# Gate products of a recurrent block: one fp32 matmul on whole tiles in place of three reduced-precision matmuls on split tiles

## The chip, the core and the metric

The kernel runs on one core of a Trainium2 chip. The metric is the device time of one execution in microseconds, as the median of several runs. A profile of one execution gives the instructions of each engine: TensorE (PE for its matmuls, PEld for its weight loads), VectorE (DVE), ScalarE (ACT), GpSimd (POOL) and SyncE (SP, which here issues the DMAs).

## What is computed

The reference is a trunk of two decoder layers on a sequence of 1024 positions with 1024 channels, all in fp32. Layer 0 mixes tokens with a gated linear recurrence (RG-LRU), layer 1 with stick-breaking attention; each is followed by a SwiGLU feed-forward network, and every sub-layer has an RMS norm before it and a residual add behind it. The change is in the recurrent block:

```python
def rg_lru_block(x, w_in, b_in, conv_w, conv_b, gate_w, gate_b, lam, w_out, b_out):
    u = jnp.einsum("bsd,de->bse", x, w_in) + b_in
    gate_branch, rec = u[..., :LRU_WIDTH], u[..., LRU_WIDTH:]
    rec = causal_depthwise_conv(rec, conv_w, conv_b)
    rec_blk = rec.reshape(bsz, seq, N_LRU_BLOCKS, LRU_BLOCK)
    gl = jnp.einsum("bsnc,gncd->gbsnd", rec_blk, gate_w).reshape(2, bsz, seq, LRU_WIDTH)
    gl = gl.astype(jnp.float32) + gate_b.astype(jnp.float32)[:, None, None, :]
    r_gate = jax.nn.sigmoid(gl[0])
    i_gate = jax.nn.sigmoid(gl[1])
    log_a = -LRU_C * r_gate * jax.nn.softplus(-lam.astype(jnp.float32))
    a = jnp.exp(log_a)
    mult = jnp.sqrt(-jnp.expm1(2.0 * log_a))
    b = mult * (i_gate * rec.astype(jnp.float32))
    _, h = lax.associative_scan(_linear_recurrence_combine, (a, b), axis=1)
    y = jax.nn.gelu(gate_branch, approximate=True) * h.astype(x.dtype)
    return jnp.einsum("bse,ed->bsd", y, w_out) + b_out
```

There are four blocks of 256 channels (N_LRU_BLOCKS, LRU_BLOCK), and the second einsum, `gl`, is two gates of four 256x256 products over all 1024 positions. It is this einsum that the change computes in another way.

## The kernel before

Activations lie with channels on the 128 partitions and positions along the free dimension, so 1024 channels are eight tiles of 128 x 1024, and a matmul moves half a tile, 512 positions, into one accumulator bank. Full precision is had from a reduced fp32 type (F32R): every operand is split into a high half, which is a cast to F32R, and a low half, the remainder, and `mm3` (lines 142 to 145) adds three matmuls, high by high, low by high and high by low. For weights, `load_raw` (line 113) brings 128 x 1024 numbers by DMA from the SP queue into one of three raw buffers (pool `rp`, tag `raw`); `split` (line 119) casts the high half on ScalarE (line 122) and subtracts for the low half on GpSimd (line 126). Both halves go into the weight ring (class `Ring`, line 67): six tiles of 128 x 1024 in two pools, four and two, handed out in turn, so that a tile is used again by the sixth allocation after it. A projection of 128 output channels takes two ring tiles and 48 matmuls (two halves, eight input tiles, three each).

The recurrent block runs its stages in the order written out in line 548, "A0 A1 B0 A2 G0 A3 Y0 B1 Y1 A4 G1 A5 B2 Y2 A6 G2 A7 B3 Y3 B4 Y4 G3 B5 Y5 B6 Y6", and `last_tile` after it. TensorE keeps this order; the other engines are ordered by a planner.

- `stage_a(e)` (line 471) projects the recurrent branch's tile e, scales it, and computes the causal convolution into `rec` (ScalarE line 478, three VectorE operations at line 480). Lines 481 to 484 split it into `rh` (ScalarE, line 482) and `rl` (VectorE, line 483); each of `rec`, `rh` and `rl` has three buffers.
- `stage_g(b)` (line 487), the gate block, covers the two channel tiles 2b and 2b+1. `load_gate` (line 442) loads both gates' weights by two DMAs into a raw buffer `rawg` (line 445) and splits them into two ring tiles. For each of two output tiles, two gates, two halves and two input tiles it calls `mm3` (line 498): 16 products, 48 matmuls, into `g_ps`. ScalarE and VectorE then do the activations and the scan of the recurrence (lines 504 to 515).
- `stage_b(e)` (line 518) projects the gate branch and applies GELU; `stage_y(e)` multiplies the two.

In each of the four gate blocks the tile `rec` is still needed after the products, at line 507. Behind the recurrent block come the output projection and the first feed-forward network, then attention and the second one; their weights go through the same ring (`wtile`, line 151), which is closed for attention (line 1352) and opened again behind it (line 1678).

Two other places use matmuls with F32 operands that aren't split: line 956 (sums of squares against a column of ones, eight products of one moving column each) and line 967 (a factor spread over the partitions, eight products of 128 moving columns); each is called once for either feed-forward network. Line 1559 in attention is a F32R matmul of 128 to 512 moving columns.

Of the kernel before, what the change touches and what calls it, by code (L numbers as in the profile page):

```python
# [8 lines left out]
F32 = mybir.dt.float32  # L9
F32R = mybir.dt.float32r  # L10
# [6 lines left out]
P = 128  # L17
S = 1024
D = 1024
# [14 lines left out]
def trunk(  # L34
# [22 lines left out]
    nc = tc.nc  # L57
    f32 = lambda t: t.bitcast(F32)

    cp = ctx.enter_context(tc.tile_pool(name="cp", bufs=1))  # L60
    rp = ctx.enter_context(tc.tile_pool(name="rp", bufs=3))
# [57 lines left out]
    def split(raw, pool=None, tag="w", bufs=None, lo_eng=None, parts=1):  # L119
        pool = pool or wpool[0]  # L120
        hi = pool.tile([P, D], F32R, tag=tag, name="whi", bufs=bufs)
        nc.scalar.copy(hi, raw)
        lo = pool.tile([P, D], F32R, tag=tag, name="wlo", bufs=bufs)
        for i in range(parts):
            c = slice(i * D // parts, (i + 1) * D // parts)
            (lo_eng or nc.gpsimd).tensor_sub(lo[:, c], raw[:, c], f32(hi)[:, c])
        return hi, lo
# [14 lines left out]
    def mm3(ps, wh, wl, mh, ml, first, last, **kw):  # L142
        nc.tensor.matmul(ps, lhsT=wh, rhs=mh, start=first, stop=False, **kw)  # L143
        nc.tensor.matmul(ps, lhsT=wh, rhs=ml, start=False, stop=False, **kw)  # L144
        nc.tensor.matmul(ps, lhsT=wl, rhs=mh, start=False, stop=last, **kw)  # L145
# [5 lines left out]
    def wtile(nm):  # L151
        return wpool[0].tile([P, D], F32R, tag="w", name=nm)
# [95 lines left out]
    half = lambda t, n: t[:, n * NB : (n + 1) * NB]  # L248
# [8 lines left out]
    with ExitStack() as st, tc.manual_schedule(engines={E.PE, E.Activation, E.DVE, E.Pool, E.SP}):  # L257
# [49 lines left out]
        ps = pst("vps0")  # L307
# [71 lines left out]
        for r0, r1 in ((0, 32), (32, 64), (64, P)):  # L379
            ps = pst("vps")  # L380
# [11 lines left out]
    with ExitStack() as st:  # L392
        lp = st.enter_context(tc.tile_pool(name="lp", bufs=1, reuse_waits="tile"))
        psl.append(lst.enter_context(tc.tile_pool(name="psB", bufs=2, space=PSUM, reuse_waits="tile")))
        V = nc.vector
        lam = vc[:, V_LAM : V_LAM + ND]
        sm = lambda name: lp.tile([P, ND], F32, name=name)
        V = nc.vector
# [38 lines left out]
        col = lambda base, i: vc[:, base + i : base + i + 1]  # L437
        ys = [lp.tile([P, S], F32, name=f"y{e}") for e in range(ND)]
        wide = lambda tag, bufs, dt=F32: lp.tile([P, S], dt, tag=tag, name=tag, bufs=bufs)
        rec, rech, recl, gel = {}, {}, {}, {}  # L440

        def load_gate(b):
            raw = rp.tile([P, D], F32, tag="raw", name="rawg")
            for g in range(2):
                nc.sync.dma_start(
                    raw[:, g * 512 : (g + 1) * 512].rearrange("p (k c) -> p k c", k=2),
                    gw[g, b].rearrange("(k p) c -> p k c", p=P),
                )
            hi, lo = split(raw)
            v4 = lambda t: t.rearrange("p (g k c) -> p g k c", g=2, k=2)  # L450
            return v4(hi), v4(lo)

        ahead = {0: aw[2], D + 2 * P: aw[3]}

# [3 lines left out]
        def ptile(name):  # L458
            turn[0] += 1
            i = (turn[0] - 1) // 2 % 2  # L460
            return psl[1 - i].tile([P, S], F32, tag="ba"[i], name=name)

        def project_col(c0):
            w = ahead.pop(c0) if c0 in ahead else load_cols(w_in, c0)
            ps = ptile("a_ps")
            for n in range(NH):
                project(ps, w, n)
            return ps


        def stage_a(e):
            ps = pa[e] if e < 2 else project_col(D + e * P)
            u = lp.tile([P, S + 16], F32, tag="u", name="u", bufs=2)
            V.tensor_copy(u[:, 0:3], nbias[:, e, 0:3])
            for n in range(NH):
                V.tensor_mul(u[:, 3 + n * NB : 3 + (n + 1) * NB], half(ps, n), rbc[n])
            rc = wide("rec", 3)
            nc.scalar.activation(rc, u[:, 3 : S + 3], AF.Identity, bias=cb[:, e : e + 1], scale=col(V_CW + 3 * ND, e))
            for j in range(3):
                V.scalar_tensor_tensor(rc, u[:, j : j + S], col(V_CW + j * ND, e), rc, op0=ALU.mult, op1=ALU.add)  # L480
            rh, rl = wide("rh", 3, F32R), wide("rl", 3, F32R)
            nc.scalar.copy(rh, rc)
            V.tensor_sub(rl, rc, f32(rh))
            rec[e], rech[e], recl[e] = rc, rh, rl


        def stage_g(b):
            gh, gl = load_gate(b)
            for i in range(2):
                e = 2 * b + i  # L490
                c = slice(i * P, (i + 1) * P)
                pss = []
                for g in range(2):
                    ps = ptile("g_ps")
                    for n in range(NH):
                        for k in range(2):
                            q = 2 * b + k
                            mm3(
                                half(ps, n), gh[:, g, k, c], gl[:, g, k, c],
                                half(rech[q], n), half(recl[q], n), k == 0, k == 1,  # L500
                            )
                    pss.append(ps)
                a, t, s = wide("ga", 2), wide("gt", 2), wide("gs", 2)
                nc.scalar.activation(a, pss[0], AF.Sigmoid, bias=col(V_GB, e))
                nc.scalar.activation(s, pss[1], AF.Sigmoid, bias=col(V_GB + ND, e))
                nc.scalar.activation(t, a, AF.Tanh, scale=ch[:, e : e + 1])
                V.tensor_mul(s, s, rec[e])
                nc.scalar.activation(a, a, AF.Exp, scale=cc[:, e : e + 1])
                V.scalar_tensor_tensor(a, a, 1.0, t, op0=ALU.add, op1=ALU.mult)
                V.scalar_tensor_tensor(a, a, 2.0, t, op0=ALU.add, op1=ALU.mult)  # L510
                V.scalar_tensor_tensor(t, a, 2.0, a, op0=ALU.add, op1=ALU.mult)
                nc.scalar.activation(t, t, AF.Sqrt, scale=-1.0)
                V.tensor_scalar_add(a, a, 1.0)
                V.tensor_mul(s, s, t)
                V.tensor_tensor_scan(ys[e], a, s, 0.0, op0=ALU.mult, op1=ALU.add)
# [31 lines left out]
        with tc.manual_schedule(engines={E.PE}):  # L547
            for what in "A0 A1 B0 A2 G0 A3 Y0 B1 Y1 A4 G1 A5 B2 Y2 A6 G2 A7 B3 Y3 B4 Y4 G3 B5 Y5 B6 Y6".split():
                {"A": stage_a, "B": stage_b, "G": stage_g, "Y": stage_y}[what[0]](int(what[1]))
            mix = last_tile(ND - 1)  # L550
# [815 lines left out]
    with ExitStack() as st:  # L1366
# [257 lines left out]
        with tc.manual_schedule(engines={E.PE, E.Activation, E.DVE, E.Pool, E.SP}):  # L1624
# [24 lines left out]
            c = 0  # L1649
# [74 lines left out]
```

## Time and profile before

| what | value |
|---|---|
| runs, median of 3 | 2180.92 us |
| lowest and highest run | 2179.82 and 2181.77 us |
| span of the profiled execution, first to last instruction | 2179.1 us |
| instructions | 27430 |
| weight loads on TensorE, busy | 1802.7 us |
| recurrent block's projections and gates | from about 39 to 237 us |

The times of the runs are of whole executions, the span is that of one profiled execution between its first and last instruction; the median stands 1.8 us above it. Busy time of an engine is the sum of its instructions' time with overlaps counted once. A matmul of 512 columns is shown 389 ns long, but the next one enters before it ends, so the pace of TensorE is read from the starts. In the lists of waits, the engine that waited stands first, behind the arrow the instruction that released it.

### The profile page before, as it was taken

Reading aid. Unit: us, or ns where it says so; the run is one execution under the profiler, and the core shown is the slowest. Engines: PE = TensorE matmul, PEld = TensorE weight load, DVE = VectorE, ACT = ScalarE, POOL = GpSimd, SP = SyncE. Lnnn points to the kernel's source line nnn. Section 1 sums busy time; section 2 is a strip of 40 time slices with the busy share of each in tenths; the row PEclk is TensorE's granted clock in tenths of the full one; section 3 lists DMA queues with packets and bytes.
Section 4 is the critical chain, followed back from the end, with each engine's and each line's share of the span. In section 5 each row is a group of like instructions: output and inputs, shape, how many; then the busy total and the mean of one; then the engine's idle time right before and its main releaser. Section 6 shows DMA issues by size and latency. Waiting matters only on the chain.

```text
span 2179.1 us, 27430 instructions
## 1 busy us (share of the span) xinstructions
PE 2165.8 (99%) x10126; PEld 1802.7 (83%) x10126; DVE 1701.4 (78%) x2380; ACT 1079.8 (50%) x1765; POOL 113.5 (5%) x85
## 2 busy tenths in 40 slices
PE   9999999999999999999999999999999999999998
PEld 7888888888888888888888888888888888888887
DVE  7888777767777887887888888886877777788886
ACT  6677445434444544564555555553543444454556
POOL 1222020000000000000000000002000000000002
PEclk9999999999999999999999999999999999999999
DMA  7111412344444764434333344552133444467452
GB/s 233 49 49 39 135 39 73 102 126 157 138 146 139 247 222 130 145 120 101 100 96 94 95 105 107 143 194 60 52 115 122 147 145 141 144 229 234 138 153 92
DMA packets 296101, 277.64 MB, mean 127 GB/s; under 512 B 15256, under 2 KB 210976, under 8 KB 295968
## 3 DMA queue, kind: packets, MB, share of 16 engines
q1 hardware_dynamic: 295808, 275.64, 40.8%
q8 instruction: 79, 1.29, 0.2%
q14 instruction: 54, 0.44, 0.1%
q10 hardware_dynamic: 160, 0.27, 0.0%
HBM read 175.71 MB, written 74.97 MB: 115 GB/s over the span
## 4 chain that ended last, share of the span: by engine, by line
PE 90%; DVE 6%; ACT 3%; DMA 1%; issue 1%; SPq 0%; DVEq 0%; ACTq 0%
PE p_ps L145 18%; PE p_ps L143 18%; PE p_ps L144 18%; PE qk_ps L143 4%; PE qk_ps L145 4%; PE qk_ps L144 4%; PE wt_ps L1538 3%; PE ob_ps L143 3%; PE ob_ps L144 2%; PE ob_ps L145 2%; PE z_ps L1508 2%; PE z_ps L1509 2%; PE av_ps L1560 2%; PE av_ps L1559 1%; PE a_ps L144 1%; PE a_ps L145 1%
## 5 line engine op out<-in xcount | busy, mean ns | idle before, releaser
L145 PE MATMUL p_ps<-vh,wal 128*128 128x512 f32 x524 | 204.1, 389 | 0.1
L143 PE MATMUL p_ps<-vh,wch 128*128 128x512 f32 x524 | 204.2, 390 | 0.0
L145 PE MATMUL p_ps<-vh,wbl 128*128 128x512 f32 x524 | 204.1, 390 | 0.0
L145 PE MATMUL p_ps<-vh,wcl 128*128 128x512 f32 x524 | 204.1, 390 | 0.0
L143 PE MATMUL p_ps<-vh,wbh 128*128 128x512 f32 x524 | 204.1, 390 | 0.0
L144 PE MATMUL p_ps<-vl,wbh 128*128 128x512 f32 x524 | 203.9, 389 | 0.0
L144 PE MATMUL p_ps<-vl,wch 128*128 128x512 f32 x524 | 203.9, 389 | 0.0
L143 PE MATMUL p_ps<-vh,wah 128*128 128x512 f32 x524 | 203.9, 389 | 0.0
L144 PE MATMUL p_ps<-vl,wah 128*128 128x512 f32 x524 | 203.9, 389 | 0.0
L1547 ACT CAST th<-wt_ps 128x512 fp32r<-128x512 f32 x192 | 92.5, 482 | 209.0 <-PE wt_ps L1538 208.8
L717 ACT CAST wbh<-sb 128x1024 fp32r<-128x1024 f32 (+2 forms) x69 | 69.8, 1011 | 192.9 <-DVE sb L701 192.9
L1548 DVE TENSOR_TENSOR tl<-wt_ps,th 128x512 fp32r<-128x512 f32 x192 | 106.0, 552 | 63.0 <-ACT th L1547 61.2
L143 PE MATMUL qk_ps<-vh,whi 128*128 128x512 f32 x264 | 118.3, 448 | 0.0
L145 PEld LDWEIGHTS p_ps<-vh,wbl 128*128 128x128 f32 x524 | 98.4, 188 | 21.4 <-DVE wbl L721 1.0
L145 PEld LDWEIGHTS p_ps<-vh,wal 128*128 128x128 f32 x524 | 98.3, 188 | 21.4 <-DVE wal L712 1.0
L145 PEld LDWEIGHTS p_ps<-vh,wcl 128*128 128x128 f32 x524 | 98.4, 188 | 21.0 <-DVE wcl L731 0.6
L143 PEld LDWEIGHTS p_ps<-vh,wch 128*128 128x128 f32 x524 | 98.4, 188 | 20.5 <-ACT tb L1106 0.2
L144 PEld LDWEIGHTS p_ps<-vl,wah 128*128 128x128 f32 x524 | 98.4, 188 | 20.4
L144 PEld LDWEIGHTS p_ps<-vl,wbh 128*128 128x128 f32 x524 | 98.4, 188 | 20.4
L144 PEld LDWEIGHTS p_ps<-vl,wch 128*128 128x128 f32 x524 | 98.4, 188 | 20.4
L143 PEld LDWEIGHTS p_ps<-vh,wah 128*128 128x128 f32 x524 | 98.4, 188 | 20.4
L143 PEld LDWEIGHTS p_ps<-vh,wbh 128*128 128x128 f32 x524 | 98.4, 188 | 20.2
(356 smaller groups left out, 5574.1 us busy)
## 6 DMA issues: line engine op xcount, KB each, us to landing
raw<-in_ffn_w_in SPq DMA_DIRECT2D x88, 512.0 KB, 3.9
vl<-pd SPq DMA_DIRECT2D x128, 256.0 KB, 3.9
pd<-U SPq DMA_DIRECT2D x90, 256.0 KB, 2.3
kk<-two SPq DMA_DIRECT2D x64, 256.0 KB, 3.9
raw<-in_ffn_w_out SPq DMA_DIRECT2D x56, 256.0 KB, 3.5
raw<-in_attn_w_qkv SPq DMA_DIRECT2D x24, 512.0 KB, 4.0
q<-two SPq DMA_DIRECT2D x64, 128.0 KB, 2.3
raw<-in_lru_w_in SPq DMA_DIRECT2D x15, 512.0 KB, 3.9
```

Source lines behind the costliest of these rows:

```text
L143: nc.tensor.matmul(ps, lhsT=wh, rhs=mh, start=first, stop=False, **kw)
L144: nc.tensor.matmul(ps, lhsT=wh, rhs=ml, start=False, stop=False, **kw)
L145: nc.tensor.matmul(ps, lhsT=wl, rhs=mh, start=False, stop=last, **kw)
L717: nc.scalar.copy(self.full(self.wb), self.full(self.sb))
L1508: nc.tensor.matmul(ps[:, 0 : c1 - c0], lhsT=lhsT, rhs=KK[q][hx][:, 0, c0:c1], start=True, stop=False)
L1509: nc.tensor.matmul(ps[:, 0 : c1 - c0], lhsT=lhsT, rhs=KK[q][hx][:, 1, c0:c1], start=False, stop=True)
L1538: nc.tensor.transpose(tp[:, c : c + P], W[q, hx, j, kb // 4][:, (kb % 4) * P : (kb % 4 + 1) * P], ident)
L1547: nc.scalar.copy(th[:, q0:], tp[:, q0:])
L1548: nc.vector.tensor_sub(tl[:, q0:], tp[:, q0:], f32(th)[:, q0:])
L1559: nc.tensor.matmul(ps[:, q0:], lhsT=VV[q][:, kb, hx], rhs=th[:, q0:], start=first, stop=False)
L1560: nc.tensor.matmul(ps[:, q0:], lhsT=VV[q][:, kb, hx], rhs=tl[:, q0:], start=False, stop=last)
```

## The change

The recurrent branch `rec` is no longer split, so the tiles `rh` and `rl` (three buffers of 4 KB a partition each) and the two instructions that write them go. The gate weights are loaded by DMA directly into one ring tile `wg`, read as F32; the raw buffer and the split on ScalarE and GpSimd go. Each product is one matmul with both operands F32. A gate block then takes one ring tile, not two, so that the kernel takes four fewer from the ring. Loop order, accumulation over two input tiles, the banks and all that comes after `g_ps` stay.

```diff
-        rec, rech, recl, gel = {}, {}, {}, {}
+        rec, gel = {}, {}
 
         def load_gate(b):
-            raw = rp.tile([P, D], F32, tag="raw", name="rawg")
+            gate = f32(wtile("wg"))
             for g in range(2):
                 nc.sync.dma_start(
-                    raw[:, g * 512 : (g + 1) * 512].rearrange("p (k c) -> p k c", k=2),
+                    gate[:, g * 512 : (g + 1) * 512].rearrange("p (k c) -> p k c", k=2),
                     gw[g, b].rearrange("(k p) c -> p k c", p=P),
                 )
-            hi, lo = split(raw)
-            v4 = lambda t: t.rearrange("p (g k c) -> p g k c", g=2, k=2)
-            return v4(hi), v4(lo)
+            return gate.rearrange("p (g k c) -> p g k c", g=2, k=2)
...
-            rh, rl = wide("rh", 3, F32R), wide("rl", 3, F32R)
-            nc.scalar.copy(rh, rc)
-            V.tensor_sub(rl, rc, f32(rh))
-            rec[e], rech[e], recl[e] = rc, rh, rl
+            rec[e] = rc
...
         def stage_g(b):
-            gh, gl = load_gate(b)
+            gate = load_gate(b)
...
-                            mm3(
-                                half(ps, n), gh[:, g, k, c], gl[:, g, k, c],
-                                half(rech[q], n), half(recl[q], n), k == 0, k == 1,
+                            nc.tensor.matmul(
+                                half(ps, n), lhsT=gate[:, g, k, c], rhs=half(rec[q], n), start=k == 0, stop=k == 1
                             )
```

## The prediction

> **What bounds the kernel now.** I read the page first, then the waits of TensorE, then the recurrent stage in windows. From the page:
>
> ```profile
> span 2179.1 us, 27430 instructions
> ...
> PE 2165.8 (99%) x10126; PEld 1802.7 (83%) x10126; DVE 1701.4 (78%) x2380; ACT 1079.8 (50%) x1765; POOL 113.5 (5%) x85
> ...
> PEclk9999999999999999999999999999999999999999
> ...
> PE 90%; DVE 6%; ACT 3%; DMA 1%; issue 1%; SPq 0%; DVEq 0%; ACTq 0%
> ```
>
> TensorE is busy 2165.8 of 2179.1 us at the full granted clock, so whatever lengthens its queue should lengthen the run. That is an average, though, and 6% of the chain of work that ended last is VectorE. The list of what TensorE and its weight loads waited for settles it:
>
> ```profile
> PE tp L314 <- DMA xt<-in_x: 3.0, 2, 1.9
> PE vps L308 <- DMA vmix<-in_mix_norm: 2.3, 1, 2.3
> PE wt_ps L1538 <- DVE tl L1548: 1.2, 3, 0.7
> PE z_ps L1508 <- DMA kk<-two: 1.1, 1, 1.1
> ```
>
> ```profile
> PEld g_ps L144 <- DVE rl L483: 0.5, 1, 0.5
> ```
>
> The columns are total us, times, longest. The waits of the matmuls themselves come to 7.6 us in the whole kernel, 5.3 of them at the start. In the recurrent block there is one wait of a weight load, 0.5 us, on the low half `rl` (line 483). Now the stage itself, 39 to 237 us, where the last row sums nine windows that alternate between plain projections and the four gate blocks (columns: length, busy us and count of PE, PEld, DVE, ACT, POOL, clock, DMA share):
>
> ```profile
> 63.00:73.90 10.90, 10.90 (x49) 9.01 (x48) 8.17 (x9) 10.29 (x10) 2.40 (x1) 1.00 0.16 48
> ...
> 193.60:204.80 11.20, 11.15 (x49) 8.93 (x48) 5.33 (x6) 9.56 (x9) 2.52 (x1) 1.00 0.15 47
> ...
> sum 198.30, PE 198.25 PEld 163.90 DVE 171.10 ACT 128.72 POOL 46.44; mean PE 22.03 PEld 18.21 DVE 19.01 ACT 14.30 POOL 5.16
> ```
>
> TensorE fills 198.25 of 198.30 us. VectorE has 27 us to spare and ScalarE 70. So the place the change touches is **bound by TensorE** and nothing that other engines save there can be seen, but for that half microsecond.
>
> **The change, part by part.** First, what TensorE loses. Each gate block issues three reduced-precision (fp32r) matmuls for each of 16 products:
>
> ```profile
> L143 PEld LDWEIGHTS g_ps<-rh,whi x64: 187/188/188, 62.8 to 203.9; 128*128 128x128 f32 x64
> L143 PE MATMUL g_ps<-rh,whi x64: 388/389/389, 63.0 to 204.1; 128*128 128x512 f32 x64
> ...
> L144 PE MATMUL g_ps<-rl,whi x64: 389/389/500, 63.3 to 204.4; 128*128 128x512 f32 x64
> ...
> L145 PE MATMUL g_ps<-rh,wlo x64: 389/389/398, 63.5 to 204.6; 128*128 128x512 f32 x64
> ```
>
> That is 192 matmuls for 64 products. The 389 ns is a length from entry to end, and neighbours overlap; what counts is start to start. The timeline of TensorE gives it, first start of a block to the first start behind it:
>
> ```profile
> 63.03 0.39 PE L143 MATMUL g_ps<-rh,whi 128*128 128x512 f32 x1
> 63.26 0.39 PE L144 MATMUL g_ps<-rl,whi 128*128 128x512 f32 x1
> ...
> 73.91 0.39 PE L143 MATMUL a_ps<-xh,whi 128*128 128x512 f32 x1
> ```
>
> ```profile
> 106.55 0.39 PE L143 MATMUL g_ps<-rh,whi 128*128 128x512 f32 x1
> ...
> 117.43 0.39 PE L143 MATMUL a_ps<-xh,whi 128*128 128x512 f32 x1
> ...
> 150.07 0.39 PE L143 MATMUL g_ps<-rh,whi 128*128 128x512 f32 x1
> ...
> 160.95 0.39 PE L143 MATMUL a_ps<-xh,whi 128*128 128x512 f32 x1
> ...
> 193.59 0.39 PE L143 MATMUL g_ps<-rh,whi 128*128 128x512 f32 x1
> ...
> 204.81 0.39 PE L143 MATMUL a_ps<-xh,whi 128*128 128x512 f32 x1
> ```
>
> Each of the first three blocks takes 10.88 us (73.91 - 63.03, and so on), 226.7 ns a matmul; the last takes 11.22, with the wait on `rl` in it. **Removed: 3 x 10.88 + 11.22 = 43.86 us.**
>
> Second, what comes instead: 64 matmuls of full fp32, moving 512 columns. The trace has no such matmul, so I bound it from smaller ones. Lines 956 and 967 are full fp32, eight products a call; line 1559 is fp32r at several widths:
>
> ```profile
> 354.78 1.84 PE L956 MATMUL ob<-ones,acc 128*128 128x1 f32 x16
> 356.48 0.49 PE L143 MATMUL p_ps<-vh,wbh 128*128 128x512 f32 x1
> ...
> 362.06 1.95 PE L967 MATMUL ob<-ident,rcol 128*128 128x128 f32 x16
> 363.76 0.48 PE L143 MATMUL p_ps<-vh,wch 128*128 128x512 f32 x1
> ```
>
> ```profile
> L956 PE MATMUL ob<-ones,acc x32: 164/250/250, 354.8 to 1561.0; 128*128 128x1 f32 x32
> ```
>
> ```profile
> L967 PE MATMUL ob<-ident,rcol x32: 271/275/275, 362.1 to 1568.4; 128*128 128x128 f32 x32
> ```
>
> ```profile
> L1559 PE MATMUL av_ps<-th,v 128*128 128x256 f32 x32 | 9.0, 282 | 0.0
> ...
> L1559 PE MATMUL av_ps<-th,v 128*128 128x128 f32 x32 | 7.2, 226 | 0.0
> ```
>
> Eight products stand as 16 records, so **one fp32 product is two records**, each with a weight load of its own. How fast does a record stream? Going from 1 to 128 columns lengthens the shortest fp32 record from 164 to 271 ns: 107 ns for 127 columns, 0.84 ns a column. For fp32r, 256 columns less 128 is 282 - 226 = 56 ns, 0.44 ns a column. So a record goes at half the fp32r rate, and a product makes four passes where the three-matmul form makes three. A record of 512 columns then streams at least 2 x 512/128 x 53.5 = 428 ns (53.5 being half of 107). The fp32r matmul takes 226.7 ns for one pass of 4 x 53.5 = 214, some 13 ns over; I take the same surplus once a record: 428 + 13 = 441, a product 0.88 us. **Added: 64 x 0.88 = 56.3 us.** Lower bound without the surplus: 64 x 0.856 = 54.8. Upper bound with the surplus on each pass: 64 x 4 x 0.2267 = 58.0.
>
> Those ends are modelled, so the rate needs another look: the 16 records of line 967 hold TensorE 1.70 us (362.06 to 363.76) and so do the 16 of one column (354.78 to 356.48), 106 ns each. At one column only the weight load can take that long, so a load costs about 106 ns and hides behind a stream; at 428 ns it hides easily. It also means that the block's length alone can't tell one pass from two, and so the first rival below keeps a chance.
>
> The Trainium skill, "FP8 and Floating Point Precision", section TensorE Precision Notes, says that true FP32 takes four passes through the array. Its sum with whole fp32r passes would be the upper bound above, with bare streams the lower one; the trace's 0.84 against 0.44 ns a column agrees.
>
> Third, the halves of `rec` and of the gate weights go:
>
> ```profile
> L482 ACT CAST rh<-rec x8: 1043/1056/1058, 51.2 to 192.3; 128x1024 fp32r<-128x1024 f32 x8
> L483 DVE TENSOR_TENSOR rl<-rec,rh x8: 1216/1218/1226, 52.4 to 193.4; 128x1024 fp32r<-128x1024 f32 x8
> ```
>
> ```profile
> L122 ACT CAST whi<-rawg x4: 1045/1052/1057, 41.3 to 173.8; 128x1024 fp32r<-128x1024 f32 x4
> L126 POOL TENSOR_TENSOR wlo<-rawg,whi x4: 2419/3370/3376, 42.4 to 177.4; 128x1024 fp32r<-128x1024 f32 x4
> ```
>
> ScalarE saves 8 x 1.06 + 4 x 1.05 = 12.7 us, VectorE 9.7, GpSimd about 12.5. All of it lies beside a TensorE that fills 198.25 of 198.30 us, so I count it as **nothing**, save that the last gate block waits for `rec` instead of `rl`, some 2.3 us earlier; its 0.34 us of stall (11.22 - 10.88) is in the 43.86 already. Next late behind that is `rec` itself, and VectorE's relief only brings it forward.
>
> Fourth, the loads. The eight gate DMAs stay on SP with the same bytes, but now they wait for TensorE to release a tile of the weight ring instead of waiting for GpSimd to release a raw buffer:
>
> ```profile
> SPq L445 <- POOL wlo L126: 26.4, 3, 11.8
> ```
>
> ```profile
> DMA to landing us min/median/max: 3.0/3.1/4.1
> ```
>
> Behind a waiting gate DMA stand the raw loads of the next projections (line 116) and behind those the splits. The ring has six tiles and a projection takes two, a gate block now one. So each block's tile is one that the third projection before it used (A1, A3, A5, A7), and is free when that one is done. Two whole projections run in between, each 48 matmuls like a gate block, 2 x 10.88 = 21.8 us, against at most 4.1 us to land and no split any more: hidden, and the next projection is due still later. Were that cover gone, a block would wait about 3.1 us, four of them 12.4 us.
>
> Fifth, four ring tiles fewer shift which of two pools later weights fall into, and 24 KB less of block-local tiles shift what later tiles overlay. The nearest rows are the longest stalls where attention starts, 1.1 us at `z_ps` above. Bounds -1.1 and +1.1, value 0, because feed-forward weights rotate through the same six tiles in the same order.
>
> **Sum:** 56.3 - 43.86 = +12.4 us, bounds 10.9 and 14.1, widened by 1.1 each way. The profiled execution's span of 2179.1 would become 2191.5. The runs' median, 2180.92, is 1.8 us above that span; I carry the 1.8 along: **2193.4 us**.
>
> **The rivals.** *Two records at fp32r speed.* If a 512-column record streams as an fp32r one does, a product costs 2 x 226.7 = 453 ns, the 64 of them 29.0 us, and the run gets **faster by 14.8 us: 2166.1**. It decides at 343 ns a record (43.86/128). For it: the two blocks of 16 records are equally long at 1 and 128 columns. Against: 164 against 271 ns. *Weight loads as the bound.* 192 loads of 188 ns become 128, 12.0 us less: 2168.9. Against: loads go every 106 ns in line 956's block. In the Trainium skill, "Trainium Kernel Development and Optimization", section Performance Expectations, LDWEIGHTS busy share, not matmul busy time, is a good metric; by that the one third of loads that goes would be a gain, which the trace so far speaks against. *Loads not hidden under fp32 streams.* 128 x 0.106 = 13.6 us more: 2207.0. Against: in line 967's block a 107 ns stream and a 106 ns load together took 106. *The gate DMA comes late:* 12.4 us more, 2205.8; against it the 21.8 us of cover. *The change doesn't do what it says:* the bitcast tiles still run in one fp32r pass, 64 x 0.2267 = 14.5 us, 29.4 less: 2151.5. Against: both operands are typed fp32, as at line 967.
>
> **How the numbers follow.** Forecast 0.87; two records at fp32r speed 0.04; weight loads as the bound 0.01; loads not hidden 0.04; late DMA 0.02; change without effect 0.01; something that cancels to within 4.4 us 0.01. A measurement of this kernel can tell about 0.2%, 4.4 us, from no change. Faster 0.06, same 0.01, slower 0.93. The forecast alone holds more than 8 in 10, so the range is its own: bounds of the sum with the shift of the ring, 2180.92 + 9.8 = 2190.7 to 2180.92 + 15.2 = 2196.1.
>
> **What would show it.** Right: 128 records on `g_ps` with 128 loads, two a product, 430 to 445 ns start to start; gate blocks of 14.1 us instead of 10.9; TensorE still without gaps from 39 us on; the rows of lines 482 and 483 and of `rawg` on GpSimd gone with no echo in the span. Wrong: records 227 ns apart (first rival), a gap in front of every record (loads exposed), TensorE waiting for a DMA into the gate tile, or a changed length of the stages behind the recurrent block.

## The result and the profile after

The changed kernel takes **2192.82 us** (median of 4 runs, 2191.86 to 2193.71) against 2180.84 us before (4 runs, 2179.82 to 2181.77). The ratio is 1.0055, with a 95% interval of 1.0042 to 1.0068: slower by 12.0 us. The prediction was 2193.4 us, range 2190.7 to 2196.1.

From the page of the changed kernel, the lines that answer to those shown of before:

```profile
span 2190.1 us, 27276 instructions
...
PE 2175.5 (99%) x10062; PEld 1789.2 (82%) x10062; DVE 1682.7 (77%) x2372; ACT 1067.3 (49%) x1753; POOL 95.7 (4%) x81
...
PE 96%; DVE 2%; ACT 1%; DMA 0%; issue 0%; DVEq 0%; SPq 0%; ACTq 0%
```

TensorE has 64 matmul records fewer (192 gone, 128 new) and is busy longer; VectorE's part of the chain that ended last falls from 6% to 2%. The windows of the changed kernel, the first gate block and then the whole recurrent stage (length, busy us and count of PE, PEld, DVE, ACT, POOL, clock, DMA share):

```profile
61.70:75.40 13.70, 13.70 (x34) 6.08 (x32) 9.48 (x10) 12.36 (x11) 2.37 (x1) 1.00 0.13 38
...
37.80:247.26 209.46, 209.46 (x813) 152.25 (x811) 155.17 (x174) 121.62 (x114) 29.58 (x12) 1.00 0.17 51
```

TensorE is without a gap here. VectorE works 155 us in 209 now, where it worked 171 in 198, and that shows nowhere in the span. The instructions on the tile `g_ps`, and the timeline of TensorE around the first gate block:

```profile
L493 PEld LDWEIGHTS g_ps<-rec,wg x128: 187/190/190, 61.5 to 213.7; 128*128 128x128 f32 x128
L493 PE MATMUL g_ps<-rec,wg x128: 590/592/593, 61.7 to 214.2; 128*128 128x512 f32 x128
```

```profile
61.71 13.89 PE L493 MATMUL g_ps<-rec,wg 128*128 128x512 f32 x32
75.04 0.79 PE L143 MATMUL a_ps<-xh,whi 128*128 128x512 f32 x1
75.68 0.40 PE L144 MATMUL a_ps<-xl,whi 128*128 128x512 f32 x1
```

One trap of reading: the projection's first matmul starts at 75.04 by the record, but it is shown 0.79 us long instead of 0.39, and its neighbour comes 0.64 us later instead of 0.23. By the record it entered early and then lasted until the last fp32 record was through. So a block is better measured to the second start behind it, 75.68 - 61.71 = 13.97 us. Before, that stretch was:

```profile
74.14 0.39 PE L144 MATMUL a_ps<-xl,whi 128*128 128x512 f32 x1
```

74.14 - 63.03 = 11.11 us. A block costs 2.86 us more. The whole gate stage runs from the first gate record to the second start behind the last block, which is, before and after:

```profile
205.04 0.39 PE L144 MATMUL a_ps<-xl,whi 128*128 128x512 f32 x1
```

```profile
214.84 0.40 PE L144 MATMUL a_ps<-xl,whi 128*128 128x512 f32 x1
```

It went from 142.01 us (63.03 to 205.04) to 153.13 (61.71 to 214.84): **+11.1 us**.

The medians differ by 12.0 us, with 9.2 to 14.8 by the interval, and the spans of the two profiled executions by 11.0; so whether 0.9 us more than the gate stage is there at all can't be told from the times. The profiles do show a longer end. The last transposes give it, before and after:

```profile
2171.72 1.95 PE L1295 MATMUL e_ps<-ident,hh 128*128 128x128 f32 x16
```

```profile
2181.72 1.94 PE L1289 MATMUL e_ps<-ident,hh 128*128 128x128 f32 x16
```

The group starts 7.4 us before the end of the span before and 8.4 after. In the same place of both kernels, 2.7 us ahead of that group, SP issues two transfers of the output, before in 0.91 us and after in 2.37:

```profile
2168.98 0.91 SPq L1309 DMA_DIRECT2D out<-y  x2
```

```profile
2178.97 2.37 SPq L1303 DMA_DIRECT2D out<-y  x2
```

Between the gate stage and that group the two kernels agree within 0.3 us. The start of the profiled execution, up to the first gate block, was 1.3 us shorter after (63.03 against 61.71); in the other profiles TensorE gets that far at 61.5 to 64.2 us, so this start varies by more than that difference.

### The profile page after: what moved, and what is told of

The parts are those of the page before. It is cut to its first block, busy times and chain, and to the rows that moved or that the text cites. A ratio compares the mean times of both kernels' runs of the same rounds, so it can differ in the third digit from the quotient of the medians.

```text
span 2190.1 us, 27276 instructions
## 1 busy us (share of the span) xinstructions
PE 2175.5 (99%) x10062; PEld 1789.2 (82%) x10062; DVE 1682.7 (77%) x2372; ACT 1067.3 (49%) x1753; POOL 95.7 (4%) x81
## 4 chain that ended last, share of the span: by engine, by line
PE 96%; DVE 2%; ACT 1%; DMA 0%; issue 0%; DVEq 0%; SPq 0%; ACTq 0%
PE p_ps L145 18%; PE p_ps L143 18%; PE p_ps L144 18%; PE qk_ps L143 4%; PE qk_ps L145 4%; PE qk_ps L144 4%; PE wt_ps L1532 3%; PE a_ps L144 3%; PE a_ps L145 3%; PE a_ps L143 3%; PE g_ps L493 3%; PE ob_ps L144 2%; PE ob_ps L143 2%; PE ob_ps L145 2%; PE z_ps L1502 2%; PE z_ps L1503 2%
```

## The experiments

All medians stand beside runs of the kernel before on the same chip, whose medians were 2180.9 to 2181.6 us. "Gate stage" is measured as above; it was 142.01 us before and 153.13 after.

| kernel | median, us | against before, 95% interval of the ratio | gate stage, us |
|---|---|---|---|
| changed again | 2192.37 | 1.0042 to 1.0067 | 153.12 |
| ring as before | 2193.32 | 1.0045 to 1.0070 | 153.12 |
| splits kept | 2193.25 | 1.0046 to 1.0071 | 153.12 |
| four passes | 2195.76 | 1.0055 to 1.0082 | 156.17 |
| twice | 2247.53 | 1.0289 to 1.0317 | 208.06 |
| half width | 2194.15 | 1.0043 to 1.0069 | 153.44 |
| bf16 passes | 2179.60 | 0.9984 to 1.0002 | 140.44 |
| late load | 2196.45 | 1.0051 to 1.0082 | 154.92, and 3.07 in front |
| high only | 2171.88 | 0.9945 to 0.9973 | 129.52 |
| high light | 2157.21 | 0.9875 to 0.9908 | 115.87 |

The theory: the four gate blocks on TensorE set the whole difference, four passes of fp32 for three of fp32r. The main rivals: part of it comes from loads, the ring or waits around the blocks; or the relief of the other engines paid back some of a larger price.

**The changed kernel again.**

> The changed kernel itself, beside the others of this call on one chip. By the theory (the four gate blocks on TensorE set the whole difference, 64 products x 0.858 us - 43.86 us = +11.1 us) it lies 11 us above before. By the rival that something behind the recurrent block adds to it, it stays at +12 us or more, and the stages behind 247 us are longer than before.

It lies 11.3 us above the runs of before beside it, its gate stage is the same to 0.01 us, and from there to the last transposes it agrees with before within 0.3 us. The longer end came back (8.6 us from the last transposes to the end of the span, before 7.4). The medians can't tell the theory's 11 us from the rival's 12.

**The ring as before.** In the changed kernel:

```diff
             gate = f32(wtile("wg"))
+            wtile("pad")
```

> The changed kernel with a second, unused ring tile per gate block, so that all later weights fall into the same ring tiles as before. Theory (the gate blocks alone): no change against the changed kernel, within 1 us, about +11 to +12 us on before. Rival (the shifted ring costs what the gate blocks don't explain, about 0.9 us): 0.9 us less than the changed kernel.

12.3 us above before; the intervals of this kernel and of the changed one overlap, and it isn't faster. The shift of the ring costs nothing that can be seen.

**Splits kept.** In the changed kernel:

```diff
+            gc = rp.tile([P, D], F32R, tag="raw", name="gc")
+            nc.scalar.copy(gc, gate)
+            nc.gpsimd.tensor_sub(gc, gate, f32(gc))
...
             rec[e] = rc
+            rh, rl = wide("rh", 3, F32R), wide("rl", 3, F32R)
+            nc.scalar.copy(rh, rc)
+            V.tensor_sub(rl, rc, f32(rh))
```

> The changed kernel with the split of rec (ScalarE and VectorE) and of the gate weights (ScalarE and GpSimd) put back, their results unread. Theory (the relief of the other engines is worth nothing): same as the changed kernel within 1 us, VectorE back up by 9.7 us and ScalarE by 12.7 us. Rival (the relief gives back part of what fp32 costs): slower than the changed kernel by a good part of 9.7 us, 2195 to 2202 us.

From the page of this kernel:

```profile
PE 2176.6 (99%) x10062; PEld 1791.1 (82%) x10062; DVE 1704.8 (78%) x2380; ACT 1079.2 (49%) x1765; POOL 110.7 (5%) x85
```

The work is back on all three engines (VectorE from 1682.7 to 1704.8 us, more than the 9.7 put back: the 24 taps of the convolution take 1.62 us each here and 1.28 in the changed kernel, among others). The gate stage is 153.12 us, the same to the hundredth. The relief is worth nothing in this kernel: shown.

**Four passes of fp32r.** In the kernel before, `mm3` with last = False, and behind it:

```diff
+                            nc.tensor.matmul(
+                                half(ps, n), lhsT=gl[:, g, k, c], rhs=half(recl[q], n), start=False, stop=k == 1
+                            )
```

> The kernel before with a fourth fp32r matmul in each gate product, low half by low half. Theory (every fp32r matmul takes 226.7 ns, an fp32 record only 429 ns for two passes): 64 x 0.2267 = +14.5 us on before, 2195.3 us, some 3 us slower than the changed kernel, which also makes four passes. Rival (four passes cost the same in either type): +11 us, level with the changed kernel.

Its timeline, first gate block:

```profile
64.17 0.39 PE L143 MATMUL g_ps<-rh,whi 128*128 128x512 f32 x1
...
78.68 0.39 PE L143 MATMUL a_ps<-xh,whi 128*128 128x512 f32 x1
```

14.51 us for 64 matmuls, 226.7 ns each. The kernel is 14.7 us slower than before and the gate stage 3.05 us longer than with fp32. So four passes in fp32r cost more than the four passes inside an fp32 product; the rival that they cost the same falls.

**Each fp32 matmul twice** (the gates' sums are doubled):

```diff
-                            nc.tensor.matmul(
-                                half(ps, n), lhsT=gate[:, g, k, c], rhs=half(rec[q], n), start=k == 0, stop=k == 1
-                            )
+                            for r in range(2):
+                                nc.tensor.matmul(
+                                    half(ps, n), lhsT=gate[:, g, k, c], rhs=half(rec[q], n),
+                                    start=k == 0 and r == 0, stop=k == 1 and r == 1,
+                                )
```

> The changed kernel with each fp32 gate matmul issued twice into the same sum, so that the gates' sums are doubled. Theory (the matmuls alone set the block's length): 64 x 0.858 = +54.9 us on the changed kernel, about 2247.5 us; blocks of 27.5 us. Rival (part of the block's 13.7 us is entry, loads or waits that come once a block): less than that, by up to 0.5 us a block and more.

```profile
63.49 27.63 PE L494 MATMUL g_ps<-rec,wg 128*128 128x512 f32 x64
...
91.18 0.40 PE L144 MATMUL a_ps<-xl,whi 128*128 128x512 f32 x1
```

The stage grows by 208.06 - 153.13 = 54.9 us, 0.858 us a product, and the run by 55 us. TensorE's time in the blocks goes into the run one to one, and nothing in a block is paid once.

**Half width.** Each fp32 matmul as two of 256 columns:

```diff
+                            for m in range(2):
+                                h = slice(n * NB + m * NB // 2, n * NB + (m + 1) * NB // 2)
...
-                                half(ps, n), lhsT=gate[:, g, k, c], rhs=half(rec[q], n), start=k == 0, stop=k == 1
+                                    ps[:, h], lhsT=gate[:, g, k, c], rhs=rec[q][:, h],
+                                    start=k == 0 and m == 0, stop=k == 1, skip_group_check=True,
```

> The changed kernel with each fp32 gate matmul of 512 columns cut into two of 256, so 256 records in place of 128. Theory (an fp32 record costs its columns at 0.417 ns twice over and some 2 ns): 256 x 0.216 = 55.3 us, +0.4 us on the changed kernel. Rival (each record costs a fixed 13 ns as an fp32r matmul does, hidden behind something in the wide form): 256 x 0.2267 = 58.0 us, +3.1 us.

```profile
63.43 13.97 PE L495 MATMUL g_ps<-rec,wg 128*128 128x256 f32 x64
...
77.47 0.40 PE L144 MATMUL a_ps<-xl,whi 128*128 128x512 f32 x1
```

The block is 14.04 us against 13.97, the stage 0.31 us longer, as the theory had it (0.4, against 3.1). The medians, 1.8 us apart with overlapping intervals, couldn't have told this; the stage can. An fp32 record has hardly any fixed cost beyond its columns.

**The passes in bf16** (the halves of `rec` and of the gate weights are held as bf16, a coarser product), in the kernel before:

```diff
-            hi, lo = split(raw)
+            hi, lo = (wtile(x).bitcast(BF16)[:, 0:D] for x in ("whi", "wlo"))
+            nc.scalar.copy(hi, raw)
+            nc.gpsimd.tensor_sub(lo, raw, hi)
...
-            rh, rl = wide("rh", 3, F32R), wide("rl", 3, F32R)
+            rh, rl = wide("rh", 3, BF16), wide("rl", 3, BF16)
```

> The kernel before with the high and low halves of the gate products held as bf16 (a coarser product), three matmuls as before. Theory (the 13 ns that an fp32r matmul takes over its 213 ns of columns come from four-byte operands, moving and weights, read at one column a cycle): about 216 ns each, 192 x 0.011 = 2.1 us less than before, 2178.7 us. Rival (every matmul pays 13 ns for the change of weights or of sum, whatever the type): same as before.

```profile
64.29 0.38 PE L143 MATMUL g_ps<-rh,whi 128*128 128x512 bf16 x1
...
65.80 0.38 PE L144 MATMUL g_ps<-rl,whi 128*128 128x512 bf16 x1
```

Seven steps from start to start in 1.51 us: 216 ns each, where fp32r takes 227. The stage is 1.57 us shorter although its last block still stalls on `rl`. The run's 2 us lie inside the interval, so the time itself is inconclusive; the pace is not.

**A late load.** In the changed kernel:

```diff
+            for _ in range(4):
+                wtile("pad")
             gate = f32(wtile("wg"))
```

> The changed kernel with four unused ring tiles taken ahead of each gate tile, so that the gate DMA must wait for the projection directly in front of the block and not for the one three back. Theory (the two projections in between hide the load): the cover is gone, each block waits 3 to 4 us for its weights, 12 to 16 us more than the changed kernel, 2205 to 2209 us. Rival (the load isn't hidden by that but would be on time anyway): no change.

The waits of TensorE in this kernel, and its timeline at block 0:

```profile
PE g_ps L495 <- DMA wg<-in_lru_gate_w: 2.7, 1, 2.7
```

```profile
61.72 0.39 PE L145 MATMUL a_ps<-xh,wlo 128*128 128x512 f32 x1
64.80 1.70 PE L495 MATMUL g_ps<-rec,wg 128*128 128x512 f32 x2 [2.68 <-DMA wg<-in_lru_gate_w]
```

Only block 0 waited. The edit didn't do what I meant in the others: their gate DMAs were issued at 91.42, 148.46 and 183.96 us, 10.9 us or more ahead of blocks that start at 112.98, 159.37 and 205.76, so that the tile they got must have been one that an earlier projection had used. So there are two prices: with no projection in between 3.07 us from start to start, where 0.23 is usual, and with one in between (10.9 us) nothing. The forecast of 12 to 16 us counted four such blocks and fails on that. But the 3.07 us aren't all. Windows of the same kernel around the wait:

```profile
58.00:61.00 3.00, 3.00 (x15) 2.49 (x14) 0.00 (x0) 0.00 (x0) 0.00 (x0) 1.00 0.00 0
61.00:64.80 3.80, 1.12 (x6) 0.61 (x5) 1.29 (x2) 2.65 (x3) 1.47 (x1) 1.00 0.39 136
64.80:67.80 3.00, 3.00 (x4) 1.27 (x5) 2.45 (x2) 2.70 (x3) 3.00 (x2) 0.56 0.19 47
```

Behind the wait the granted clock is 0.56 for 3 us, and the block takes 1.8 us more (154.92 against 153.12 over the stage).

**High halves alone** (the low halves don't enter the products), in the kernel before:

```diff
-                            mm3(
-                                half(ps, n), gh[:, g, k, c], gl[:, g, k, c],
-                                half(rech[q], n), half(recl[q], n), k == 0, k == 1,
+                            nc.tensor.matmul(
+                                half(ps, n), lhsT=gh[:, g, k, c], rhs=half(rech[q], n), start=k == 0, stop=k == 1
                             )
```

> The kernel before with the gate products from the high halves alone (the low halves are still made, but unread), one fp32r matmul in place of three. If TensorE alone bounds the recurrent stage: 128 x 0.2267 = 29.0 us less than before, 2151.8 us. Rival (VectorE, with 171 us of work in the 198 us of the stage, becomes the bound as soon as TensorE gives up 27 us, and its chains earlier): a gain of 15 to 25 us only, with TensorE waiting for rec, rl or a free bank in the stage.

29.0 us of TensorE's work taken away bring 9.2 us. Both expectations fail in size, the first altogether. Waits and windows of this kernel:

```profile
PE g_ps L498 <- ACT rh L482: 8.6, 3, 4.6
```

```profile
99.00:104.17 5.17, 0.61 (x3) 0.19 (x1) 5.17 (x5) 1.08 (x2) 2.66 (x1) 0.77 0.12 32
104.17:109.00 4.83, 4.83 (x11) 3.47 (x11) 3.67 (x6) 4.79 (x5) 0.00 (x0) 0.54 0.25 76
142.80:145.25 2.45, 0.38 (x2) 0.00 (x1) 2.01 (x5) 1.08 (x2) 0.00 (x0) 1.00 0.00 0
145.25:149.00 3.75, 3.75 (x11) 2.90 (x11) 2.51 (x3) 3.72 (x4) 0.27 (x1) 0.62 0.00 0
```

TensorE arrives at blocks 1 to 3 before `rh` is there, waits 2 to 5 us, in which VectorE is busy most of the time (5.17 of 5.17 us, 2.01 of 2.45), and comes back at a lower clock: 0.54 and 0.62 in the stretches behind the waits, with matmuls 427 ns apart instead of 227. The stage falls by 12.5 us only, and the output projection behind it grows by 2.3 (89.31 against 87.04).

**High light.** The same without making the low halves at all (GpSimd's subtraction for the gate weights and VectorE's `rl` go):

```diff
-            hi, lo = split(raw)
+            hi = wtile("whi")
+            nc.scalar.copy(hi, raw)
...
             nc.scalar.copy(rh, rc)
-            V.tensor_sub(rl, rc, f32(rh))
```

> The kernel before with the gate products from the high halves alone, and the low halves of rec and of the gate weights not made at all: as in the run with high halves alone (9.2 us less than before), but with VectorE relieved of 9.7 us and GpSimd of 12.5. Theory (once TensorE gives up more than VectorE can follow, VectorE's work on the gates' chain sets the stage, and relief counts): 15 to 19 us less than before, 2162 to 2166 us. Rival (what holds that run back is latency between engines or the clock after idle time, not VectorE's work): 9 to 11 us less, as without the relief.

```profile
PE g_ps L498 <- DVE u L477: 2.1, 1, 2.1
```

23.7 us less than before, 14.5 more than the high halves alone gave beside their own runs of before. The relief (9.7 us of VectorE's work, 12.5 of GpSimd's, and one ring tile fewer a block) is worth more here than VectorE's part of it is long, while in the changed kernel the relief of the other engines was worth nothing. From the first gate record to the output projection, with high halves alone and then in this kernel:

```profile
62.88:224.84 161.96, 152.14 (x642) 122.72 (x640) 141.77 (x119) 117.47 (x108) 37.02 (x14) 0.96 0.17 49
```

```profile
62.48:210.78 148.30, 146.20 (x642) 119.81 (x640) 130.16 (x113) 121.35 (x111) 30.47 (x11) 1.00 0.18 54
```

Of the 13.7 us between them, 7.7 are idle time of TensorE (9.8 against 2.1), and 5.9 are the same 642 matmuls taking longer at a mean granted clock of 0.96. So the theory of this run holds in sign and is exceeded in size, because the lower clock that the rival named went away together with the waits. What VectorE's relief, GpSimd's and the ring tile are worth each wasn't separated.

## Why the prediction was right

- **The bound.** Right for work added to TensorE: 54.9 us more gave 55 us more. The other half of the sentence, that VectorE "has 27 us to spare", was a mean and doesn't hold as a margin: with 29 us of TensorE's work gone the run gained 9.2, because TensorE then waited for the chain to `rh` and ran at a lower clock behind the waits.
- **The 43.86 us removed** is confirmed by the blocks' pace, which the four-pass kernel repeats at 226.7 ns.
- **Two records a product, four passes**: 128 records on `g_ps` with 128 loads. The Trainium skill, "FP8 and Floating Point Precision", section TensorE Precision Notes, has four passes for true FP32; the 0.858 us of a product are four times 214.5 ns, so the trace agrees. The rivals with a record at fp32r's pace, with one fp32r pass a product, with loads as the bound or exposed, fall with it: records stand 429 ns apart and TensorE has no gap. The rate of 0.84 ns a column rested on the shortest records (164 and 271 ns); the middle ones of the same lines (250 and 275) would have given 0.2. Nothing in the trace of before showed which to take; the 429 ns for 512 columns bear out the shortest.
- **The size of the product was off.** I put 441 ns on a record, carrying over the 13 ns by which an fp32r matmul exceeds its columns. A record takes 429, just under the 430 to 445 that I gave as the sign of being right. So 54.9 us were added and not 56.3: the lower bound of the term, 54.8, was the right one. Added less removed is 11.07 us, as the gate stage shows. The 106 ns for a weight load was also a little off, by the trap described above: in the blocks of lines 956 and 967 the loads stand 111 to 112 ns apart by their own starts.
- **The sum came out closer than its terms.** 12.0 us were measured and 12.5 forecast, but the gate blocks, which were the whole of the forecast, give only 11.1. That the number came so close is luck: the runs don't resolve a microsecond, and the longer end, 1.0 us in the profile, was in no term of the sum.
- **The relief at nothing**: shown by the kept splits.
- **The gate DMA**: SP waits for TensorE's release as I said, and lands in time:

```profile
SPq L445 <- PE a_ps L145: 25.2, 4, 7.7
```

```profile
DMA to landing us min/median/max: 2.7/3.2/4.1
```

- The price of a lost cover, put at 3.1 us a block, was 2.8 us of waiting (3.07 less the usual 0.23) in the one block that lost it, and 1.8 more behind the wait, at the lower clock. **The ring at nothing**: nothing that the runs can tell.

Open: why the last stretch is about a microsecond longer. The profiles of all runs whose recurrent stage grew have it, 0.7 to 1.5 us, those whose stage shrank don't. Each profile that has it shows among SP's last twelve issues of the output at least one that takes 1.03 to 2.42 us; in the others none takes more than 0.44. Why such an issue is held up, and what it has to do with the length of the recurrent stage, isn't shown.

## What to carry to other kernels

A single fp32 product takes the time of four passes and a split product makes three, so trading one for the other cost 858 ns for 680 on an engine that is full, whatever it spared the others; count passes and the pace from starts, not instructions. Relief of engines that aren't the bound was worth nothing, until the bound itself gave way: not making the low halves was worth 0 in one kernel and 14.5 us in another. A mean over the stage showed that work on the bound would lengthen the run, but not how much could be taken from the bound.

## What the runs showed of the hardware that I had not expected

Moving 512 columns, an fp32r matmul takes 226.7 ns from start to start, a bf16 one 216, and each pass inside an fp32 record 214.5. The 11 to 13 ns belong to fp32r and not to the number of records (half-width fp32 records stay at 216 ns for two passes of 256). Bf16 differs in its weight loads too, 98 ns long instead of 188, so whether the moving operand or the load makes the difference is open.

A wait of TensorE can cost more than itself: behind gaps of 4.95, 2.46 and 2.33 us from start to start (high halves alone) and 3.07 us (late load) the granted clock is 0.54 to 0.62 over the next 3 to 5 us. The Trainium skill, "TensorE: Matmul & The Clock Gate", section Part 1: The HAM clock gate, describes a clock that falls to half after an idle window of about 3.4 us and returns after a busy one. The traces agree with the half (behind the late load the fp32 records start 853 ns apart instead of 429, and then 429 again) and with the return. They show no fixed length of gap that brings it about: 2.33 us were enough in one place, and in high light a gap of 2.49 us (101.50 to 103.99 us) was followed by a granted clock of 1.00.
